# Stick-breaking attention on one core: the diagonal mask moved from a matmul into the scan, and eight small products moved from VectorE to ScalarE

## The chip, the cores and the metric

The kernel runs on one core of a Trainium2 chip, in one launch. The metric is the device time in microseconds. Three runs of the kernel before took 1741.11, 1733.97 and 1735.38 us, so the median is 1735.38 us.

The engines are named as the profile names them: PE is TensorE, with PEld for its weight loads; DVE is VectorE; ACT is ScalarE; POOL is GpSimd; SP is SyncE, which issues the DMAs here. `DVEq` or `SPq` is the part of an engine that issues instructions.

## The reference, cut to what matters

One decoder layer over 2048 positions of 1024 features, all in float32. A conditioning vector `c` gives shift, scale and gate; the input is normalised and modulated, projected to 4096 columns, and goes through eight heads of stick-breaking attention and four heads of differential attention. Each head's output is gated, everything is joined, projected back and added to `x`.

```python
mod = c @ w_ada + b_ada                       # 3 x 1024: shift, scale, gate
h = rmsnorm(x, norm_g) * (1 + scale) + shift

# stick-breaking head, query t, key s:
z = (q @ k.T) / 8
mask = s < t                                  # strictly causal
log_1m = where(mask, log_sigmoid(-z), 0)
rem = reverse_cumsum(log_1m) - log_1m         # sum over s < j < t
a = where(mask, exp(log_sigmoid(z) + rem), 0)
out = a @ v
```

So the weight of key `s` is sigmoid(z) at `s` times the product of sigmoid(-z) over all keys strictly between `s` and `t`. Keys at `t` and behind it have weight zero.

## The kernel before, in words

**Precision.** Each matmul operand is split into a rounded part (`hH`, `wh`, `aH`: fp32r) and the rest (`hL`, `wl`, `aL`), and each product is three matmuls (`mm3`, L381 to L383). Scores are built from stored high and low parts of q and k in two matmuls (L547).

**Start.** The 1024 features are taken in eight blocks `k` of 128. For each block DVE forms 128 values of scale and 128 of shift as dot products of rows of `w_ada` with `c` (`ada_block`, L179, two instructions of 512 columns for each 128 values). Then `gmul[k] = (1 + scale) * norm_g` (L1015) is made on DVE. PE transposes the normalised `x` (L304), ACT multiplies by `gmul` and adds the shift (L310), ACT rounds that to `hH` (L311), POOL (for `k` from 1 to 6) or DVE (0 and 7) takes the rest `hL` (L312), and PE adds block `k` into four projection tiles `ps_p` and `ps_k` (12 matmuls of 512 columns).

**Stick-breaking heads.** The sequence is done in two halves of 1024 queries. For each head, a block `i` of 128 queries is a row of work over `L = (i + 1) * 128` keys, taken in segments of up to 512 keys from the last to the first (`front`, L653 on). The last segment, called `top` in the code, holds the diagonal block as its last 128 columns. A segment is: the scores into a PSUM tile `ps_z`; a sigmoid of them by ACT into `s` (L680); a sigmoid of their negative by ACT in place (L681); on DVE a scan from right to left that multiplies up the second sigmoid into `u` (L684), begun at one in the top segment and at the next segment's left end in the others; and on POOL `s[j] *= u[j + 1]` (L688). For the diagonal, a third matmul (L550, `identr` times `maskr`) adds -1e30 to the scores of keys at or behind the query: there the first sigmoid is zero and the second is one. `maskr` is built once on POOL in `more_constants`. With eight heads and 16 blocks there are 128 such rows, 320 segments and 128 mask matmuls. For two rows together `s` is then transposed by PE (L583), split, and multiplied with `v` (L665, L666).

**Order.** A planner weaves the attention steps with the steps of the projections (lists `A` and `P`, costs beside each step), and a scheduler then sets the order on each engine. The `big` pool has six buffers of 2048 columns for `u` and `s` (and, in the differential heads, `e0` and `e1`). `dist` is a table in SBUF, with zero or negative distances and -1e30, that the differential heads add; the scan names it as its second input and passes it by.

Of the kernel before, what the change touches and what calls it, by code (L numbers as in the profile page):

```python
# [8 lines left out]
F32R = mybir.dt.float32r  # L9
I32 = mybir.dt.int32  # L10
AF = mybir.ActivationFunctionType
ALU = mybir.AluOpType
# [4 lines left out]
T = 2048  # L17
# [7 lines left out]
OUT_SCALE = 0.8  # L25
KAPPA_CAP = 2.0 ** 100
NBIG = 6
MASKED = -1e30
NSTG = 8
WINDOW = 17.0  # L30
QK_DELAY = 3
# [15 lines left out]
def build(ctx: ExitStack, tc, xT, xN, cT, cK, normg, w_adaT, b_ada, w_in, qg, kg, lam4, subg, w_out,  # L47
          identd, distd, outT):
    nc = tc.nc
# [12 lines left out]
    def ctile(shape, name, dt=F32):  # L62
        return cpool.tile(shape, dt, name=name, tag=name)
# [16 lines left out]
    identr = ctile([128, 128], "ident", F32R)  # L80
# [9 lines left out]
    ngt = ctile([128, KT], "ngt")  # L90
# [1 line left out]
    qgt = ctile([128, 1], "qgt")  # L92
    kgt = ctile([128, 1], "kgt")
    sgt = ctile([128, 1], "sgt")
    dist = ctile([128, T], "dist")
    maskr = ctile([128, 128], "maskr", F32R)
    qgain = ctile([128, NDF], "qgain")
    subg8 = ctile([128, 1], "subg8")
    ldot = ctile([128, 2], "ldot")
# [3 lines left out]
    def more_constants():  # L103
        nc.sync.dma_start(qgt, qg)
        nc.sync.dma_start(kgt, kg)
        nc.sync.dma_start(sgt, subg)
        tmp0 = ppool.tile([128, 512], F32, name="tmp0", tag="stg", bufs=NSTG)
        lamt = tmp0[:, 0:256].rearrange("p (f d) -> p f d", d=64)
        nc.sync.dma_start(lamt, lam4.unsqueeze(0).broadcast_to([128, 4, 64]))
        for h in range(NDF):  # L110
            nc.gpsimd.tensor_scalar(out=qgain[:, h:h + 1], in0=qgt, scalar1=0.125 / SLOPES[h],
                                    scalar2=None, op0=ALU.mult)
        nc.gpsimd.tensor_scalar(out=subg8, in0=sgt, scalar1=OUT_SCALE, scalar2=None, op0=ALU.mult)
        lprod = tmp0[:, 256:384].rearrange("p (f d) -> p f d", d=64)
        nc.vector.tensor_tensor(out=lprod, in0=lamt[:, 0::2, :], in1=lamt[:, 1::2, :], op=ALU.mult)
        nc.vector.reduce_sum(out=ldot, in_=lprod, axis=AX.X)
        nc.scalar.activation(lexp, ldot, AF.Exp)
        nc.vector.tensor_tensor(out=neglam, in0=lexp[:, 1:2], in1=lexp[:, 0:1], op=ALU.subtract)
        nc.vector.tensor_scalar(out=neglam, in0=neglam, scalar1=-LAM_INIT, scalar2=None, op0=ALU.add)
        mk = tmp0[:, 384:512]  # L120
        nc.gpsimd.memset(mk, 0.0)
        nc.gpsimd.affine_select(out=mk, in_=mk, pattern=[[-1, 128]], compare_op=ALU.is_gt,
                                fill=MASKED, base=0, channel_multiplier=1)
        nc.gpsimd.tensor_copy(maskr, mk)


    def dtile(shape, name):
# [29 lines left out]
    def after(ins, f):  # L157
        with tc.issue_after(ins.ins):
            return f()
# [8 lines left out]
    mod = ctile([128, 24], "mod")  # L168
# [5 lines left out]
    def ada_block(third, j, wt, cb):  # L174
        m = third * 8 + j
        part = col.tile([128, 1], F32, name="part", tag="adas", bufs=1)
        for i, (ini, acc) in enumerate(((badat[:, m:m + 1], part), (part, mod[:, m:m + 1]))):
            ws = wt[:, i * 512:i * 512 + 512]
            nc.vector.tensor_tensor_reduce(out=ws, in0=ws, in1=cb[i], scale=1.0, scalar=ini,  # L179
                                           op0=ALU.mult, op1=ALU.add, accum_out=acc)  # L180
# [34 lines left out]
    gmul = ctile([128, KT], "gmul")  # L215
# [86 lines left out]
    def turn(ps, xn, k):  # L302
        for t in range(4):
            nc.tensor.transpose(ps[:, t * 128:(t + 1) * 128],  # L304
                                xn[k // 4][t][:, (k % 4) * 128:(k % 4) * 128 + 128], ident)
# [169 lines left out]
    last_pe = [None]  # L475
# [64 lines left out]
                              src[u % 2, :, :, qs:qs + 256].rearrange("l p t -> p l t"))  # L540
        return qt

    def scores(q, kch, i, k0, w, diag=None):
        ps = zps.tile([128, 512], F32, name="ps_z", tag="z")
        tl = slice((i % 2) * 128, (i % 2) * 128 + 128)
        for pt in range(2):
            last_pe[0] = nc.tensor.matmul(ps[:, :w], lhsT=q[:, pt, tl], rhs=kch[k0 // 512][:, :w],  # L547
                                          start=pt == 0, stop=pt == 1 and diag is None)
        if diag is not None:
            last_pe[0] = nc.tensor.matmul(ps[:, diag:diag + 128], lhsT=identr, rhs=maskr, start=False,  # L550
                                          stop=True)
        return ps

    def segs(n, ext):
        return [(o, min(512, n - o), min(512, n - o)) for o in range(0, n, 512)]
# [91 lines left out]
    class SBHead(Head):  # L647
# [20 lines left out]
        def front(self, i, A):  # L668
            steps = []
            tiles = {}  # L670

            def step(c0, w, we, first):
                self.open()
                q = self.get_q(i // 2)
                if first:
                    tiles["u"], tiles["s"] = self.row("u", i), self.row("s", i)
                u, s = tiles["u"], tiles["s"]
                dg = i * 128 - c0
                ps = scores(q, self.kch, i, c0, we, dg if 0 <= dg < w else None)
                nc.scalar.activation(s[:, c0:c0 + w], ps[:, :w], AF.Sigmoid, scale=0.125)  # L680
                nc.scalar.activation(ps[:, :w], ps[:, :w], AF.Sigmoid, scale=-0.125)  # L681
                top = c0 + w == L
                ur = ps[:, :w][:, ::-1]
                nc.vector.tensor_tensor_scan(out=u[:, c0:c0 + w][:, ::-1], data0=ur, data1=dist[:, :w],  # L684
                                             initial=1.0 if top else u[:, c0 + w:c0 + w + 1],
                                             op0=ALU.mult, op1=ALU.bypass)
                m = w - 1 if top else w
                nc.gpsimd.tensor_tensor(out=s[:, c0:c0 + m], in0=s[:, c0:c0 + m],  # L688
                                        in1=u[:, c0 + 1:c0 + m + 1], op=ALU.mult)

            L = (i + 1) * 128
            ext = (i // 2 + 1) * 256
            for si, (c0, w, we) in enumerate(reversed(segs(L, ext))):
                steps.append((2 * w / 960, lambda c0=c0, w=w, we=we, f=si == 0: step(c0, w, we, f)))

            def mid():
                A[0] = tiles["s"]
            return steps, (0.2, mid)
# [313 lines left out]
    turn(xps[0], xn0, 0)  # L1012
    for k in range(KT):
        after(rs0, lambda: ada_block(1, k, wa[(1, k)], cb))
        nc.vector.scalar_tensor_tensor(out=gmul[:, k:k + 1], in0=mod[:, 8 + k:9 + k], scalar=1.0,  # L1015
                                       in1=ngt[:, k:k + 1], op0=ALU.add, op1=ALU.mult)
        after(rs0, lambda: ada_block(0, k, wa[(0, k)], cb))
        make_h(k, 0, xps[k % 2], *hs[0], k in POOL_H)
        if k + 1 < KT:
            turn(xps[(k + 1) % 2], xn0, k + 1)  # L1020
        for w, pst in ((w_q, pq), (w_k, pk)):
            for s in range(2):
                wh, wl = w[k]
                ws = slice(s * 128, s * 128 + 128)
                mm3(pst[s], wh[:, ws], wl[:, ws], hs[0][0][(k, 0)], hs[0][1][(k, 0)], k == 0,
                    k == KT - 1)
# [220 lines left out]
def _layout(inputs):  # L1247
    import numpy as np
    a = {k: np.asarray(v) for k, v in inputs.items()}
    p = np.arange(128)  # L1250
    j = np.arange(T)
    rel = (j[None, :] - 1920 - p[:, None]).astype(np.float32)
    return {
        "xT": np.ascontiguousarray(a["x"][0].T),
        "xN": np.ascontiguousarray(a["x"][0]),
        "cT": np.ascontiguousarray(a["c"][0]),
        "cK": np.ascontiguousarray(a["c"][0].reshape(KT, 128).T),
        "normg": np.ascontiguousarray(a["norm_g"][0].reshape(KT, 128).T),
        "w_adaT": np.ascontiguousarray(a["w_ada"][0].T),
        "b_ada": np.ascontiguousarray(a["b_ada"][0].reshape(24, 128).T),  # L1260
        "w_in": np.ascontiguousarray(a["w_in"][0]),
        "qg": np.ascontiguousarray(np.tile(a["q_norm_g"][0], 2).reshape(128, 1)),
        "kg": np.ascontiguousarray(np.tile(a["k_norm_g"][0], 2).reshape(128, 1)),
        "lam4": np.ascontiguousarray(np.stack([a["lambda_q1"][0], a["lambda_k1"][0],
                                               a["lambda_q2"][0], a["lambda_k2"][0]])),
        "subg": np.ascontiguousarray(a["subln_g"][0].reshape(128, 1)),
        "w_out": np.ascontiguousarray(a["w_out"][0]),
        "ident": np.eye(128, dtype=np.float32),
        "dist": np.where(rel <= 0, rel, np.float32(-1e30)).astype(np.float32),
    }  # L1270


# [18 lines left out]
```

## Time and profile before

| what | before |
|---|---|
| median of 3 runs | 1735.38 us |
| the profiled execution, whole | 1733.63 us |
| its span, first to last instruction | 1731.8 us |
| mean granted TensorE clock | 0.996 |
| PE busy | 1669.4 us, 96% |
| DVE busy | 1236.3 us, 71% |
| ACT busy | 1000.3 us, 58% |
| POOL busy | 836.6 us, 48% |
| DMA | 268.15 MB, mean 155 GB/s |

The span is the time inside which all rows below lie; the profiled execution took 1.8 us more. The profile counts an instruction as busy from its start to the end of its result, and matmuls are pipelined, so the next one starts before the last has ended. What a matmul takes from the engine is therefore read from the distance between starts.

### The profile page before, as it was taken

The page shows a single profiled execution, that of the slowest core. Times are in us where ns is not written, and L with a number is a line of the kernel's source. Part 1 is how long each engine was busy: PE and PEld are TensorE (multiplying, and loading weights), DVE is VectorE, ACT ScalarE, POOL GpSimd, SP SyncE. Part 2 cuts the span into 40 slices and gives each one's busy share as a digit, 9 for nine tenths or more (in the row PEclk, how much of TensorE's full clock was granted, in tenths as well). Part 3 has the DMA queues.
Part 4 walks back from the last instruction along what each step waited for, and adds up shares of the span by engine and source line. Part 5 has one row for each costly group of instructions (what it writes and reads, how often), then busy time and mean ns, then how long its engine had stood idle before and what let it go on. Part 6 is the DMA issues. An engine that isn't in the chain of part 4 may idle for free.

```text
span 1731.8 us, 31619 instructions
## 1 busy us (share of the span) xinstructions
PE 1669.4 (96%) x10816; PEld 1494.2 (86%) x10816; DVE 1236.3 (71%) x2556; ACT 1000.3 (58%) x2027; POOL 836.6 (48%) x1266
## 2 busy tenths in 40 slices
PE   7899899999999999999999999999999999999999
PEld 6688688899999889878898889899998978888887
DVE  6626455766566887767787887788788889888741
ACT  4625555456555454766776777687665645554521
POOL 3325455457545644655565465576332353223553
PEclk9999999999999999999999999999999999999999
DMA  9585767534654975434432332234433566443264
GB/s 348 167 236 162 199 201 240 184 108 117 200 169 142 286 211 163 149 107 117 128 116 89 102 98 86 80 104 126 132 99 108 164 208 200 128 134 129 88 220 149
DMA packets 212690, 268.15 MB, mean 155 GB/s; under 512 B 21424, under 2 KB 136368, under 8 KB 212400
## 3 DMA queue, kind: packets, MB, share of 16 engines
q1 hardware_dynamic: 212528, 266.12, 50.5%
q8 instruction: 86, 1.41, 0.3%
q14 instruction: 76, 0.62, 0.1%
HBM read 186.34 MB, written 79.69 MB: 154 GB/s over the span
## 4 chain that ended last, share of the span: by engine, by line
PE 64%; DVE 8%; DMA 4%; issue 4%; POOL 3%; ACT 3%; SPq 1%; DVEq 0%; ACTq 0%; POOLq 0%
PE ps_z L547 10%; PE ps_t L583 8%; PE ps_n L381 5%; PE ps_n L383 5%; PE ps_n L382 5%; PE ps_p L381 4%; PE ps_p L383 4%; PE ps_p L382 4%; PE av L666 3%; PE av L665 3%; PE ps_o L381 3%; PE ps_o L382 3%; PE ps_o L383 3%; DMA xt<-in_xT 2%; DVE u L684 1%
## 5 line engine op out<-in xcount | busy, mean ns | idle before, releaser
L688 POOL TENSOR_TENSOR s<-s,u 128x512 f32<-128x512 f32 (+4 forms) x320 | 306.2, 959 | 274.1 <-DVE u L684 238.5
L547 PE MATMUL ps_z<-kc,qc 128*128 128x512 f32 (+3 forms) x1280 | 358.8, 374 | 10.5 <-DVE u L684 7.9
L589 ACT CAST aH<-ps_t 128x512 fp32r<-128x512 f32 (+1 forms) x432 | 240.7, 567 | 168.7 <-PE ps_t L583 165.1
L590 DVE TENSOR_TENSOR aL<-ps_t,aH 128x512 fp32r<-128x512 f32 (+1 forms) x432 | 276.7, 650 | 79.7 <-ACT aH L589 78.3
L369 POOL TENSOR_TENSOR wl<-raw,wh 128x512 fp32r<-128x512 f32 x168 | 224.5, 1344 | 128.1 <-ACT wh L365 118.3
L381 PE MATMUL ps_n<-wh,hH 128*128 128x256 f32 x960 | 275.2, 287 | 2.5 <-DVE sl L392 2.2
L383 PE MATMUL ps_n<-wh,hL 128*128 128x256 f32 x960 | 271.6, 283 | 0.0
L382 PE MATMUL ps_n<-wl,hH 128*128 128x256 f32 x960 | 271.2, 283 | 0.4 <-POOL wl L369 0.4
L684 DVE TENSOR_TENSOR_SCAN u<-ps_z,u,dist 128x512 f32<-128x512 f32 x192 | 245.7, 1280 | 32.2 <-ACT ps_z L681 26.5
L780 ACT ACTIVATE e<-e,nm 128x1024 f32<-128x1024 f32 (+4 forms) x192 | 172.1, 898 | 125.3 <-DVE nm L778 121.0
L547 PEld LDWEIGHTS ps_z<-kc,qc 128*128 128x128 f32 x1280 | 210.8, 190 | 37.4 <-DVE u L684 13.4
L766 DVE CUSTOM_DVE_ANT_0 e<-ps_z,dist 128x512 f32<-128x512 f32 (+3 forms) x320 | 186.6, 604 | 50.8 <-PE ps_z L547 44.0
L680 ACT ACTIVATE s<-ps_z 128x512 f32<-128x512 f32 (+3 forms) x320 | 172.9, 540 | 77.4 <-PE ps_z L547 39.2
L381 PE MATMUL ps_p<-hH,wh 128*128 128x512 f32 x480 | 192.2, 406 | 6.1 <-ACT hH L311 6.1
L382 PE MATMUL ps_p<-hL,wh 128*128 128x512 f32 x480 | 190.5, 397 | 0.8 <-POOL hL L312 0.6
L383 PE MATMUL ps_p<-hH,wl 128*128 128x512 f32 x480 | 189.3, 394 | 0.0
L381 PEld LDWEIGHTS ps_n<-wh,hH 128*128 128x128 f32 x960 | 182.6, 191 | 7.0 <-DVE sl L392 2.5
L382 PEld LDWEIGHTS ps_n<-wl,hH 128*128 128x128 f32 x960 | 182.7, 191 | 3.7 <-POOL wl L369 0.6
L383 PEld LDWEIGHTS ps_n<-wh,hL 128*128 128x128 f32 x960 | 182.8, 191 | 1.8
L681 ACT ACTIVATE ps_z<-ps_z 128x512 f32<-128x512 f32 (+3 forms) x320 | 173.5, 542 | 0.0
L583 PE MATMUL ps_t<-ident,s 128*128 128x128 f32 x1088 | 168.6, 275 | 4.6 <-DVE aL L590 4.3
L665 PE MATMUL av<-aH,vc 128*128 128x256 f32 x576 | 160.7, 290 | 7.9 <-ACT aH L589 6.7
(190 smaller groups left out, 3456.0 us busy)
## 6 DMA issues: line engine op xcount, KB each, us to landing
qc<-qst SPq DMA_DIRECT2D x256, 128.0 KB, 3.1
raw<-in_w_in SPq DMA_DIRECT2D x120, 256.0 KB, 3.2
kc<-kst SPq DMA_DIRECT2D x96, 256.0 KB, 3.5
vc<-vst SPq DMA_DIRECT2D x48, 256.0 KB, 3.0
vc<-vdt SPq DMA_DIRECT2D x48, 256.0 KB, 3.6
raw<-in_w_out SPq DMA_DIRECT2D x48, 256.0 KB, 3.4
wada<-in_w_adaT SPq DMA_DIRECT2D x16, 512.0 KB, 8.3
qst<-sh SPq DMA_DIRECT2D x64, 128.0 KB, 2.5
```

Of the source, the lines that this page charges most:

```text
L369: (eng or nc.gpsimd).tensor_tensor(out=wl, in0=raw, in1=wh.bitcast(F32), op=ALU.subtract)
L381: nc.tensor.matmul(ps, lhsT=aH, rhs=bH, start=first, stop=False)
L382: nc.tensor.matmul(ps, lhsT=aH, rhs=bL, start=False, stop=False)
L383: nc.tensor.matmul(ps, lhsT=aL, rhs=bH, start=False, stop=last)
L547: last_pe[0] = nc.tensor.matmul(ps[:, :w], lhsT=q[:, pt, tl], rhs=kch[k0 // 512][:, :w], start=pt == 0, stop=pt == 1 and diag is None)
L583: nc.tensor.transpose(tp[:, pos * 256 + t * 128:pos * 256 + t * 128 + 128], A[t][0][:, sb * 128:sb * 128 + 128], ident)
L589: nc.scalar.copy(aH[:, f0:], tp[:, f0:])
L590: nc.vector.tensor_tensor(out=aL[:, f0:], in0=tp[:, f0:], in1=aH[:, f0:].bitcast(F32), op=ALU.subtract)
L665: nc.tensor.matmul(o, lhsT=v, rhs=aH, start=st, stop=False)
L684: nc.vector.tensor_tensor_scan(out=u[:, c0:c0 + w][:, ::-1], data0=ur, data1=dist[:, :w], initial=1.0 if top else u[:, c0 + w:c0 + w + 1], ...
L688: nc.gpsimd.tensor_tensor(out=s[:, c0:c0 + m], in0=s[:, c0:c0 + m], in1=u[:, c0 + 1:c0 + m + 1], op=ALU.mult)
L766: nc.vector.tensor_tensor_reduce(out=e[m][:, c0 + o:c0 + o + w], in0=ps[:, :w], in1=dist[:, d0:d0 + w], scale=1.0, scalar=-3e38, op0=ALU.a ...
```

## The change

The mask matmul, its constant and the three POOL instructions that build it go. The scan of a top segment gets a second operation: after the multiplication it takes the maximum with an input, and it begins at zero instead of one. That input is read backwards from `dist`, which is 128 columns longer; those columns are an identity matrix. From the right, the product stays zero until the diagonal, where the maximum with the identity's one makes it one, and from there it is the product as before. The other columns of `dist` that are read are zero or negative and change nothing. So `u` is zero behind the diagonal, and `s * u` is zero there whatever `s` is. The very last column of a row has no `u` to its right: ACT now leaves it out (511 columns of 512, and so on), and POOL writes a zero there (a memset of 128 x 1, one for each of the 128 rows). Apart from that, the eight `gmul` products are made by ACT (identity of scale times `ngt` plus `ngt`) instead of by DVE.

```diff
-    dist = ctile([128, T], "dist")
-    maskr = ctile([128, 128], "maskr", F32R)
+    dist = ctile([128, T + 128], "dist")
...
-        mk = tmp0[:, 384:512]
-        nc.gpsimd.memset(mk, 0.0)
-        nc.gpsimd.affine_select(out=mk, in_=mk, pattern=[[-1, 128]], compare_op=ALU.is_gt,
-                                fill=MASKED, base=0, channel_multiplier=1)
-        nc.gpsimd.tensor_copy(maskr, mk)
...
-    def scores(q, kch, i, k0, w, diag=None):
+    def scores(q, kch, i, k0, w):
...
-                                          start=pt == 0, stop=pt == 1 and diag is None)
-        if diag is not None:
-            last_pe[0] = nc.tensor.matmul(ps[:, diag:diag + 128], lhsT=identr, rhs=maskr, start=False,
-                                          stop=True)
+                                          start=pt == 0, stop=pt == 1)
...
-                dg = i * 128 - c0
-                ps = scores(q, self.kch, i, c0, we, dg if 0 <= dg < w else None)
-                nc.scalar.activation(s[:, c0:c0 + w], ps[:, :w], AF.Sigmoid, scale=0.125)
+                ps = scores(q, self.kch, i, c0, we)
+                top = c0 + w == L
+                m = w - 1 if top else w
+                nc.scalar.activation(s[:, c0:c0 + m], ps[:, :m], AF.Sigmoid, scale=0.125)
+                if top:
+                    nc.gpsimd.memset(s[:, L - 1:L], 0.0)
...
-                nc.vector.tensor_tensor_scan(out=u[:, c0:c0 + w][:, ::-1], data0=ur, data1=dist[:, :w],
-                                             initial=1.0 if top else u[:, c0 + w:c0 + w + 1],
-                                             op0=ALU.mult, op1=ALU.bypass)
+                nc.vector.tensor_tensor_scan(out=u[:, c0:c0 + w][:, ::-1], data0=ur,
+                                             data1=dist[:, T + 128 - w:T + 128][:, ::-1] if top else dist[:, :w],
+                                             initial=0.0 if top else u[:, c0 + w:c0 + w + 1],
+                                             op0=ALU.mult, op1=ALU.max if top else ALU.bypass)
...
-        nc.vector.scalar_tensor_tensor(out=gmul[:, k:k + 1], in0=mod[:, 8 + k:9 + k], scalar=1.0,
-                                       in1=ngt[:, k:k + 1], op0=ALU.add, op1=ALU.mult)
+        nc.scalar.activation(gmul[:, k:k + 1], mod[:, 8 + k:9 + k], AF.Identity,
+                             scale=ngt[:, k:k + 1], bias=ngt[:, k:k + 1])
...
-        "dist": np.where(rel <= 0, rel, np.float32(-1e30)).astype(np.float32),
+        "dist": np.concatenate([np.where(rel <= 0, rel, np.float32(-1e30)),
+                                j[None, :128] == p[:, None]], axis=1).astype(np.float32),
```

The scheduler sets the order anew. Three places show what stands where. The first is DVE at the start, where block `k` = 3 of the modulation is formed (`ISA` with `mod` as its result ends 128 values; `wada` is a tile of `w_ada` rows, `ps_cb` holds `c`). Before:

```order
L179 ISA wada_255,part_463<-wada_255,ps_cb_213,badat_109 128x512
L179 ISA part_463 128x1
L179 ISA wada_255,mod_195<-wada_255,ps_cb_214,part_463 128x512
L179 ISA mod_195 128x1
L1015 SCALAR_TENSOR_TENSOR gmul_196<-mod_195,ngt_111 128x1
L179 ISA wada_255,part_467<-wada_255,ps_cb_213,badat_109 128x512
L179 ISA part_467 128x1
L179 ISA wada_255,mod_195<-wada_255,ps_cb_214,part_467 128x512
```

DVE at the same place in the changed kernel:

```order
L174 ISA wada_254,part_462<-wada_254,ps_cb_212,badat_109 128x512
L174 ISA part_462 128x1
L174 ISA wada_254,mod_194<-wada_254,ps_cb_213,part_462 128x512
L174 ISA mod_194 128x1
L174 ISA wada_254,part_466<-wada_254,ps_cb_212,badat_109 128x512
L174 ISA part_466 128x1
L174 ISA wada_254,mod_194<-wada_254,ps_cb_213,part_466 128x512
```

The product `gmul` no longer stands between the values of scale and those of shift; on ACT it now stands ahead of L310 of the same block, eight times.

The second is PE where the first three rows of the first head are scored, between matmuls of a projection. Before:

```order
L382 MATMUL ps_p<-hL_0_558,wh 128x512
L547 MATMUL ps_z<-kc,qc 128x128 x2
L550 MATMUL ps_z<-maskr,ident 128x128
L547 MATMUL ps_z<-kc,qc 128x256 x2
L550 MATMUL ps_z<-maskr,ident 128x128
L547 MATMUL ps_z<-kc,qc 128x384 x2
L550 MATMUL ps_z<-maskr,ident 128x128
L383 MATMUL ps_p<-hH_0_557,wl 128x512
```

PE at the same place in the changed kernel:

```order
L377 MATMUL ps_p<-hL_0_557,wh 128x512
L542 MATMUL ps_z<-kc,qc 128x128 x2
L542 MATMUL ps_z<-kc,qc 128x256 x2
L542 MATMUL ps_z<-kc,qc 128x384 x2
L378 MATMUL ps_p<-hH_0_556,wl 128x512
```

Only the mask matmuls have gone there; elsewhere in the stick-breaking stretches steps have traded places with their neighbours, and the differential heads and the end of the program stand as before.

The third is POOL in the second half, where row `s_11956` (before) or `s_11950` (changed kernel) ends a head and `s_12071` or `s_12065` begins the next one. Before:

```order
L688 TENSOR_TENSOR s_11874<-s_11874,u_11873 128x383
L688 TENSOR_TENSOR s_11874<-s_11874,u_11873 128x512 x2
L688 TENSOR_TENSOR s_11956<-s_11956,u_11955 128x511
L688 TENSOR_TENSOR s_11956<-s_11956,u_11955 128x512 x2
L714 TENSOR_TENSOR ot_12017<-ot_12017,gt_12015 64x512
L688 TENSOR_TENSOR s_12071<-s_12071,u_12070 128x127
```

POOL at the same place in the changed kernel:

```order
L683 TENSOR_TENSOR s_11868<-s_11868,u_11867 128x383
L683 TENSOR_TENSOR s_11868<-s_11868,u_11867 128x512 x2
L675 MEMSET s_11950 128x1
L675 MEMSET s_12065 128x1
L683 TENSOR_TENSOR s_11950<-s_11950,u_11949 128x511
L683 TENSOR_TENSOR s_11950<-s_11950,u_11949 128x512 x2
L709 TENSOR_TENSOR ot_12011<-ot_12011,gt_12009 64x512
L683 TENSOR_TENSOR s_12065<-s_12065,u_12064 128x127
```

The memset of the next row stands ahead of the products of the row before it, and it waits for PE to have transposed what its buffer held last.

## Rows read from the trace of the kernel before

**Rows 1.** The page: engine, busy us (share of the span), instructions.

```profile
PE 1669.4 (96%) x10816; PEld 1494.2 (86%) x10816; DVE 1236.3 (71%) x2556; ACT 1000.3 (58%) x2027; POOL 836.6 (48%) x1266
```

**Rows 2.** Two stick-breaking stretches: length, busy us per engine, clock, DMA share, GB/s.

```profile
200.00:420.00 220.00, 208.64 (x1372) 187.83 (x1370) 134.80 (x210) 121.26 (x257) 119.29 (x151) 1.00 0.57 170
860.00:1060.00 200.00, 198.56 (x1292) 177.83 (x1290) 157.38 (x191) 145.30 (x294) 111.02 (x107) 1.00 0.33 102
```

**Rows 3.** Who PE waited for: us in total, times, longest us.

```profile
PE ps_z L547 <- DVE u L684: 7.9, 15, 0.8
PE ps_t L583 <- DVE aL L590: 6.7, 10, 2.4
PE av L665 <- ACT aH L589: 6.7, 6, 1.4
```

**Rows 4.** The mask matmul by form: count, busy us, mean ns, idle us before.

```profile
L550 PE MATMUL ps_z<-maskr,ident 128*128 128x128 f32 x128 | 30.4, 237 | 0.0
```

**Rows 5.** PE's timeline around a mask matmul: start us, us, instruction.

```profile
118.53 0.22 PE L550 MATMUL ps_z<-maskr,ident 128*128 128x128 f32 x1
118.59 0.45 PE L383 MATMUL ps_p<-hH,wl 128*128 128x512 f32 x1
118.88 0.39 PE L381 MATMUL ps_p<-hH,wh 128*128 128x512 f32 x1
119.10 0.40 PE L382 MATMUL ps_p<-hL,wh 128*128 128x512 f32 x1
```

**Rows 6.** PE's timeline behind scores without a mask matmul.

```profile
901.10 0.63 PE L547 MATMUL ps_z<-kc,qc 128*128 128x512 f32 x2
901.57 0.28 PE L382 MATMUL ps_n<-wl,hH 128*128 128x256 f32 x1
901.69 0.27 PE L383 MATMUL ps_n<-wh,hL 128*128 128x256 f32 x1
```

**Rows 7.** The product gmul: its durations (min/median/max ns), and DVE and POOL once.

```profile
L1015 DVE SCALAR_TENSOR_TENSOR gmul<-mod,ngt x8: 159/1286/1292, 17.0 to 47.3; 128x1 f32<-128x1 f32 x8
25.50 1.29 DVE L1015 SCALAR_TENSOR_TENSOR gmul<-mod,ngt 128x1 f32<-128x1 f32 x1
25.48 1.29 POOL L312 TENSOR_TENSOR hL<-xh,hH 128x512 fp32r<-128x512 f32 x1 [5.88 <-ACT hH L311]
```

**Rows 8.** PE's timeline at the start: transposes, first matmuls of blocks 2 and 7.

```profile
29.18 0.66 PE L304 MATMUL ps_x<-ident,xn 128*128 128x128 f32 x4
...
29.83 0.73 PE L381 MATMUL ps_p<-hH,wh 128*128 128x512 f32 x2
...
51.99 0.73 PE L381 MATMUL ps_p<-hH,wh 128*128 128x512 f32 x2 [1.23 <-ACT hH L311]
```

**Rows 9.** The tile wada up to 60 us: its issues on SP, and issue to landing.

```profile
L172 SPq DMA_DIRECT2D wada<-in_w_adaT x16: 328/340/668, 6.6 to 29.0; - x16
...
DMA to landing us min/median/max: 4.8/8.3/9.5
```

**Rows 10.** DVE by form: a top scan, and a plain subtraction of the same shape.

```profile
L590 DVE TENSOR_TENSOR aL<-ps_t,aH 128x512 fp32r<-128x512 f32 x336 | 225.4, 680 | 65.7 <-ACT aH L589 64.8
...
L684 DVE TENSOR_TENSOR_SCAN u<-ps_z,dist 128x512 f32<-128x512 f32 x32 | 38.9, 1215 | 8.8 <-ACT ps_z L681 6.3 <-PE ps_t L583 2.4
```

**Rows 11.** A small memset on POOL, and a small activation on ACT.

```profile
L1278 POOL MEMSET const-float32-0.0<- 128x1 f32 x1 | 0.1, 98 | 0.2 <-issue 0.2
L117 ACT ACTIVATE lexp<-ldot 128x2 f32<-128x2 f32 x1 | 0.2, 203 | 2.8 <-DVE ldot L116 2.8
```

**Rows 12.** What POOL waited for most: us in total, times, longest us.

```profile
POOL s L688 <- DVE u L684: 238.5, 196, 8.1
```

**Rows 13.** Timelines of PE and POOL where a buffer comes free.

```profile
910.88 0.60 PE L583 MATMUL ps_t<-ident,s 128*128 128x128 f32 x4
...
912.25 0.63 POOL L688 TENSOR_TENSOR s<-s,u 128x255 f32<-128x255 f32 x1 [3.22 <-DVE u L684]
```

**Rows 14.** ACT's timeline: an activation that waits for a DMA.

```profile
104.20 0.63 ACT L220 ACTIVATE xacc<-xt 128x512 f32<-128x512 f32 x1 [5.81 <-DMA xt<-in_xT]
```

More of the change, by code (lines that the diff above doesn't have):

```diff
@@ L27 @@
 NBIG = 6
-MASKED = -1e30
 NSTG = 8
@@ L677, in step @@
                 u, s = tiles["u"], tiles["s"]
-                dg = i * 128 - c0
-                ps = scores(q, self.kch, i, c0, we, dg if 0 <= dg < w else None)
-                nc.scalar.activation(s[:, c0:c0 + w], ps[:, :w], AF.Sigmoid, scale=0.125)
+                ps = scores(q, self.kch, i, c0, we)
[4 more added lines that the diff above has]
+                    nc.gpsimd.memset(s[:, L - 1:L], 0.0)
                 nc.scalar.activation(ps[:, :w], ps[:, :w], AF.Sigmoid, scale=-0.125)
-                top = c0 + w == L
                 ur = ps[:, :w][:, ::-1]
-                nc.vector.tensor_tensor_scan(out=u[:, c0:c0 + w][:, ::-1], data0=ur, data1=dist[:, :w],
-                                             initial=1.0 if top else u[:, c0 + w:c0 + w + 1],
-                                             op0=ALU.mult, op1=ALU.bypass)
-                m = w - 1 if top else w
+                nc.vector.tensor_tensor_scan(out=u[:, c0:c0 + w][:, ::-1], data0=ur,
+                                             data1=dist[:, T + 128 - w:T + 128][:, ::-1] if top else dist[:, :w],
+                                             initial=0.0 if top else u[:, c0 + w:c0 + w + 1],
+                                             op0=ALU.mult, op1=ALU.max if top else ALU.bypass)
                 nc.gpsimd.tensor_tensor(out=s[:, c0:c0 + m], in0=s[:, c0:c0 + m],
```

## The prediction

> **What bounds the kernel now.** Read the page's busy line first: PE is busy 96% of the span, DVE 71%, ACT 58%, POOL 48% [rows 1]. A busy share can hide stalls, since a matmul counts as busy until its result is out. So look next at the table by stretch: in a stretch of stick-breaking rows of the first half PE is busy 208.64 of 220 us, in one of the second half 198.56 of 200, DVE 134.80 and 157.38 [rows 2]. Last, who PE waited for: the three largest are 7.9, 6.7 and 6.7 us in the whole run, 31 waits together [rows 3]. PE is the bound, from the first scores to the end, and what leaves its queue shortens the run unless a wait stands right behind it. The other place is the start, up to about 55 us, where PE waits for each block of the modulated input.
>
> **The mask matmuls on PE.** There are 128, with a mean duration of 237 ns [rows 4], but the duration is not the price. The timeline shows one start at 118.53, the next matmul at 118.59 and the one behind that at 118.88 [rows 5]. So the mask matmul holds the queue 0.06 us, and the 512-column matmul behind it needs 0.29 us until the next start where the following one of the same shape needs 0.22 (118.88 to 119.10): another 0.07. Behind plain scores nothing is stretched: at 901.57 a 256-column matmul gives way after 0.12 us [rows 6], about half of what 512 columns take. [...] That is 0.13 us, with rounding at four ends; I take 0.12, so 128 x 0.12 = 15.4 us. What PE saves just ahead of a wait, the wait eats: with 31 waits I take off 31 x 0.12 = 3.7. That leaves 11.7 us. Bounds: 15.4 where no wait eats any, and 128 x 0.06 = 7.7 less a quarter for waits, 5.8, where the stretch stays and goes to the matmul before.
>
> [...]
>
> **The product gmul at the start.** It works on one column, but its median is 1286 ns against a least of 159 [rows 7]. The reason stands beside it: at 25.50 it begins while POOL runs `hL` from 25.48 for 1.29 us, and it ends with it. While it stands there, the shift of the same block, next on DVE, is late; ACT's L310 waits for that shift, and PE for ACT. PE's first matmul of block 2 starts at 29.83 and that of block 7 at 51.99, so one block takes 22.16 / 5 = 4.43 us; at block 7 PE had waited 1.23 us [rows 8]. PE's own work for a block is four transposes, 0.66 us [rows 8], and 12 matmuls at 0.22 us [rows 5], 3.3 us. DVE without the product needs about 4.43 - 1.29 = 3.1 us a block. So PE becomes the pace, with 4.43 - 3.3 = 1.13 us gained on each of five blocks: 5.6 us. The loads allow it: the last `wada` issue is at 29.0, and with a landing after at most 9.5 us all are there at 38.5 [rows 9], where the new pace wants the last block at about 45. On ACT the product costs about 0.2 us by a small activation [rows 11]; ACT waits for DVE there anyway. I take 5.0 of the 5.6, since behind the blocks come loads that no engine paces: at 104.20 ACT has waited 5.81 us for a DMA of `xt`, with other work queued behind it [rows 14]. Bounds: 5.6, and 0 where those loads take back all of it.
>
> [...]
>
> **The scan with a maximum.** No row shows a scan whose second operation does anything. A top scan of 512 takes 1215 ns, a subtraction of the same shape 680 [rows 10], so the scan already pays nearly two steps for each element, as a loop through two operations would, although the second is passed by. I take the price of the maximum as zero. Bounds: below nothing there is no reason; above, a third step, (1215 / 2) = 0.6 us per 512 columns. The 32 top segments of each width hold 32 x (128 + 256 + 384 + 512) = 40,960 columns, 80 times 512, so 48 us on DVE.
>
> **POOL's memsets.** 128 at about 0.1 us [rows 11] are 12.5 us on POOL, which waited 238.5 us for scans in these rows [rows 12]; they fit there. Where that cover is gone they cost at most the 12.5. They also add a wait: in the second half the memset of the next row stands ahead of the products of the row before and waits for PE to have transposed its buffer's last content. Behind it stand those products, and PE's next transposes wait for these. The trace shows when that buffer comes free: four transposes start at 910.88 and end at 911.48, and the product behind them starts at 912.25, since its scan needs the same buffers [rows 13]. So the memset has 0.8 us before the product is due. I take nothing; up to 0.1 us a row, 64 rows, 6 us above, and nothing below. The mask's three POOL instructions (once) and one column less for ACT are nothing either way: both engines wait there.
>
> **The sum.** 11.7 + 5.0 = 16.7 us off the profiled execution, 1733.63, is 1716.9. It stands 1.75 us below the median of the runs, so the forecast for a median is 1718.6. The 1.8 us around the span stay.
>
> **The rivals.** First, the start's gain is given back, so that only PE's 11.7 stays: 1735.38 - 11.7 = 1723.7. For it: the first scores come at 118, behind stores, reloads and the DMA waits of rows 14. Against it: most of those loads are issued when PE or DVE is done with something, and would shift along.
>
> Second, the rows of attention don't run at PE's pace but at that of the chain from ACT's sigmoids over the scan to POOL's product; PE would only wait more, and the start's 5.0 is all: 1730.4. For it: POOL's 238.5 us of waiting for scans, and 11 us of PE idle in 220 in the first half [rows 2]. Against it: PE's named waits are only 21 us in all, and the chain gets shorter by 0.06 us a row too, since ACT's sigmoid waited for the mask.
>
> Third, on the other side: the maximum makes top scans slower by a third step, 48 us on DVE in the stretches where it is busy 61% to 79%. If all of it ends up in PE's waits, the time is 1735.38 - 16.7 + 48 = 1766.7; it decides (slower by over 0.5%) once PE waits for more than 25 of the 48. Against it: the scan's rate already is that of two operations.
>
> [...]
>
> Fourth, the change doesn't do what it says because the new order, made for the changed set of instructions, loses elsewhere what it gains: I put 10 us on that, 1728.6. For it: steps have traded places in the stick-breaking stretches. Against it: most move by one or two matmuls.
>
> **How the numbers follow.** Forecast 0.62, 1711 to 1726 by the bounds (15.4 + 5.6 = 21.0 with 3 us for waits that vanish below; 5.8 + 3.0 above). First rival 0.12, second 0.12, third 0.06, fourth 0.08. For 8 in 10 the range reaches from 1710 to 1731, over the first, second and most of the fourth. Half a per cent, 8.7 us, is what a measurement of this kernel can tell from none; the border is 1726.7. Faster by more: the forecast, most of the first rival, a little of the fourth: 0.74. Within: the second, most of the fourth, part of the third: 0.19. Slower: most of the third and bad orders: 0.07.
>
> **What would show it.** The PE work without L550 has the same spacing, and matmuls behind scores no longer show 0.29 us. At the start, blocks follow each other on PE every 3.3 us, DVE's dot products have no gap of 1.2 us, and the first scores start before 114 us instead of about 118. A top scan of 512 still takes about 1.2 us. POOL's memsets take 0.1 us, and POOL's products start no later behind their scans. I am wrong if PE's waits for DVE or ACT grow by more than the 3.7 us taken off, if the first scores still start near 118, or if the top scans take 1.8 us.

## The result, and the profile after

The changed kernel took 1727.47 us in the median of six runs (1724.80 to 1730.57), the kernel before 1736.70 us in six runs beside them. The ratio is 0.9945, with an interval from 0.9927 to 0.9963: 9.2 us faster. Six more runs of the changed kernel (e9) gave 0.9952 (0.9933 to 0.9971) beside runs of the kernel before. The forecast was 1718.6 us, so a little over half of the forecast gain arrived. The profiled execution took 1727.51 us, with a span of 1725.7 us.

The first fence is the page of the changed kernel, the line that answers to [rows 1].

```profile
PE 1659.9 (96%) x10688; PEld 1482.5 (86%) x10688; DVE 1231.1 (71%) x2548; ACT 1005.4 (58%) x2035; POOL 847.2 (49%) x1391
```

The 128 mask matmuls are gone from PE, ACT has eight instructions more and DVE eight less, POOL has 125 more. Next, two stretches of the changed kernel, moved by about 10 us against [rows 2]: length, busy us of PE, PEld, DVE, ACT and POOL, granted clock, DMA share, GB/s.

```profile
190.00:410.00 220.00, 210.64 (x1338) 187.96 (x1338) 138.41 (x211) 124.72 (x261) 121.26 (x192) 0.98 0.59 173
850.00:1050.00 200.00, 195.52 (x1240) 171.77 (x1239) 155.69 (x190) 142.36 (x290) 112.68 (x130) 1.00 0.32 100
```

In the first stretch PE is as busy as before. In the second it isn't: it is idle 200 - 195.52 = 4.5 us, where the kernel before was idle 1.4 us [rows 2]. The clock column matters too: 0.98 in the first stretch, where the kernel before showed 1.00. Now the start, on PE of the changed kernel: first matmuls of blocks 2 and 7 (start us, us, instruction), and the eight `gmul` products, now on ACT (duration ns min/median/max, first and last start).

```profile
29.45 0.71 PE L376 MATMUL ps_p<-hH,wh 128*128 128x512 f32 x2
...
45.53 0.61 PE L376 MATMUL ps_p<-hH,wh 128*128 128x512 f32 x2
```

```profile
L1010 ACT ACTIVATE gmul<-mod,ngt x8: 382/387/389, 17.9 to 41.6; 128x1 f32<-128x1 f32 x8
```

Five blocks take 45.53 - 29.45 = 16.1 us, 3.2 us each, where they took 4.43 [rows 8]. The product takes 0.39 us on ACT, and nobody waits for it there. Then DVE's top scan and POOL's memsets of the changed kernel, by form (count, busy us, mean ns, idle us before and what ended it), and POOL's wait at the memsets.

```profile
L679 DVE TENSOR_TENSOR_SCAN u<-ps_z,dist 128x512 f32<-128x512 f32 x32 | 38.9, 1217 | 12.5 <-ACT ps_z L676 12.3
```

```profile
L675 POOL MEMSET s<- 128x1 f32 x128 | 10.4, 100 | 35.4 <-PE ps_t L575 34.2
```

```profile
POOL s L675 <- PE ps_t L575: 34.2, 12, 7.0
```

The scan with the maximum takes 1217 ns, without it 1215 [rows 10]. The memsets take 0.1 us each, and twelve of them wait, up to 7.0 us. Whether that wait costs anything the page can't say; run e11 below does. Last, PE at the place of [rows 5], in the changed kernel:

```profile
110.93 0.97 PE L542 MATMUL ps_z<-kc,qc 128*128 128x128 f32 x6
111.74 0.39 PE L378 MATMUL ps_p<-hH,wl 128*128 128x512 f32 x1
111.97 0.39 PE L376 MATMUL ps_p<-hH,wh 128*128 128x512 f32 x1
112.20 0.40 PE L377 MATMUL ps_p<-hL,wh 128*128 128x512 f32 x1
```

The matmul behind the scores needs 0.23 us until the next start, as the one behind it does (111.97 to 112.20); the 0.29 us are gone. The first scores start at 110.93 instead of 117.50. PE's named waits for DVE and ACT come to 51.0 us in the whole run, where they were 50.4, so the prediction's sign of being wrong (more than 3.7 us more) doesn't show in them.

### The profile page after: what moved, and what is told of

Same layout as the page of the kernel before. It is cut to its first block, busy times and chain, and to the rows that moved or that the text cites. A ratio compares the mean times of both kernels' runs of the same rounds, so it can differ in the third digit from the quotient of the medians.

```text
span 1725.7 us, 31468 instructions
## 1 busy us (share of the span) xinstructions
PE 1659.9 (96%) x10688; PEld 1482.5 (86%) x10688; DVE 1231.1 (71%) x2548; ACT 1005.4 (58%) x2035; POOL 847.2 (49%) x1391
## 4 chain that ended last, share of the span: by engine, by line
PE 68%; DVE 11%; DMA 7%; issue 5%; ACT 4%; POOL 4%; SPq 1%; DVEq 0%; ACTq 0%; POOLq 0%
PE ps_z L542 11%; PE ps_t L575 7%; PE ps_n L376 6%; PE ps_n L378 6%; PE ps_n L377 6%; PE ps_p L376 4%; PE ps_p L377 4%; PE ps_p L378 4%; DVE u L679 3%; PE ps_o L377 3%; PE ps_o L376 3%; PE ps_o L378 3%; PE av L658 3%; PE av L657 3%; DMA xt<-in_xT 3%
## 5 line engine op out<-in xcount | busy, mean ns | idle before, releaser
L673 ACT ACTIVATE s<-ps_z 128x512 f32<-128x512 f32 (+4 forms) x320 | 169.2, 543 | 67.2 <-PE ps_z L542 48.9
L676 ACT ACTIVATE ps_z<-ps_z 128x512 f32<-128x512 f32 (+3 forms) x320 | 168.2, 538 | 1.8
```

## The experiments

**How the runs are compared.** Each run lists its mean granted clock. Over the 173 runs of all kernels in these experiments, a run whose mean clock is 0.001 lower is 1.03 us longer (a fit with one level for each kernel; 0.88 to 1.19). The kernels differ by a few us and the runs of one kernel by ten, so the table gives each kernel's time at a clock of 0.994 from this fit, with its 95% interval, beside the plain median. "Old" is the order of instructions that the kernel before has, "new" that of the changed kernel.

| kernel | order | runs | median us | mean clock | at 0.994, us |
|---|---|---|---|---|---|
| before (e1 and beside all others) | old | 85 | 1737.8 | 0.9936 | 1737.2 ± 0.5 |
| e2, gmul on ACT alone | old | 9 | 1728.4 | 0.9942 | 1729.8 ± 1.4 |
| e5, masks gone alone | old | 5 | 1730.1 | 0.9928 | 1728.9 ± 1.9 |
| e8, e10, the whole change | old | 12 | 1723.5 | 0.9939 | 1723.1 ± 1.2 |
| changed kernel, with e9 | new | 12 | 1728.6 | 0.9910 | 1726.1 ± 1.3 |
| e3, without gmul on ACT | new | 12 | 1735.9 | 0.9927 | 1732.8 ± 1.2 |
| e11, memsets moved | new | 8 | 1729.6 | 0.9910 | 1726.6 ± 1.6 |
| e6, masks put back | new | 12 | 1739.1 | 0.9916 | 1735.1 ± 1.3 |
| e7, the same work | a third | 12 | 1734.2 | 0.9904 | 1730.9 ± 1.3 |
| e4, without memsets | a fourth | 6 | 1727.7 | 0.9938 | 1727.7 ± 1.7 |

**The kernel before again.** My theory after this profile was that the gain at the start had arrived, that the mask matmuls gave little, and that a denser PE had lost some 5 us to a lower clock. No edit.

> The kernel before, unchanged, run again: its own granted clock is wanted. In the profiled runs the clock was 0.996 before and 0.993 after; the six runs of after lay between 0.990 and 0.993. Theory A (the lower clock belongs to the change, a denser PE): all runs of the kernel before show 0.995 or more, and the time stays at 1736.7 us within 0.2%. Rival B (how often the clock falls is chance in either kernel): the runs of the kernel before spread over 0.990 to 0.996 like those of after, and the slower of them are those with the lower clock.

Median 1736.56 us of 12 runs, clock from 0.989 to 0.998. The kernel before falls to low clocks too, and its runs with a low clock are the long ones: the five at 0.993 or less took 1738.98 to 1742.89 us, the seven at 0.995 or more 1731.37 to 1736.98. So the time of a single profiled run may not be read for a few us: that of the kernel before, at 0.996, was a lucky one. Theory A is out as it stands: low clocks aren't the change's alone. Whether they are more frequent in the changed kernel is taken up at the end.

**The parts alone.** e2 is the kernel before with the `gmul` products on ACT:

```diff
-        nc.vector.scalar_tensor_tensor(out=gmul[:, k:k + 1], in0=mod[:, 8 + k:9 + k], scalar=1.0,
-                                       in1=ngt[:, k:k + 1], op0=ALU.add, op1=ALU.mult)
+        nc.scalar.activation(gmul[:, k:k + 1], mod[:, 8 + k:9 + k], AF.Identity,
+                             scale=ngt[:, k:k + 1], bias=ngt[:, k:k + 1])
```

> The kernel before with the eight gmul products on ACT, mask matmul and scan as they were; PE, POOL and SP run in the same order as before. Theory A (the start gave what it was forecast, and it lasts to the end): 4.9 us less, about 1731.8 us, first scores at about 111 us. Rival 1 of the prediction (the start's gain is given back to loads behind it): first scores near 111, but the offset to the kernel before is gone by 300 us, time within 1 us of 1736.7. If a kernel with less waiting at the start pays in granted clock, the clock falls to about 0.993 here too.

Ratio 0.9956 (0.9938 to 0.9974): 8.8 us by medians, 7.4 at equal clock, more than the 4.9 expected. These rows are the scores in the kernel before and then in e2, first at their beginning and then at their end (duration ns, first and last start us, forms):

```profile
L547 PE MATMUL ps_z<-kc,qc x11: 220/335/499, 117.5 to 124.8; 128*128 128x128 f32 x4, 128*128 128x512 f32 x3, 128*128 128x256 f32 x2, 128*128 128x384 f32 x2
L547 PE MATMUL ps_z<-kc,qc x28: 333/396/496, 1602.9 to 1623.5; 128*128 128x512 f32 x24, 128*128 128x384 f32 x4
```

```profile
L547 PE MATMUL ps_z<-kc,qc x14: 220/320/477, 111.6 to 124.1; 128*128 128x128 f32 x4, 128*128 128x256 f32 x4, 128*128 128x512 f32 x4, 128*128 128x384 f32 x2
L547 PE MATMUL ps_z<-kc,qc x22: 333/396/500, 1601.4 to 1618.1; 128*128 128x512 f32 x20, 128*128 128x384 f32 x2
```

The first scores come 5.9 us earlier, the last 5.4 us. The start's gain lasts, and the first rival is out. For e3 the same edit is undone in the changed kernel:

> The changed kernel with the gmul products back on DVE: mask by the scan alone; PE and POOL run in the order of the changed kernel. Theory A (start 4.9, the mask matmuls net 4.3 of the 11.7 forecast): about 1732.4 us, clock between 0.990 and 0.993, first scores near 117.5. Rival (the mask matmuls gave their 11.7 and the start gave nothing in the end): about 1727 here, as in the changed kernel with both. Rival 4 (the new order costs): can't be told apart here, the order stays.

1735.87 us, ratio 0.9983 (0.9968 to 0.9999): 1.4 us by medians, 4.4 at equal clock. The theory's number was 1732.4, the rival's 1727; neither is met by the median, and at equal clock (1732.8) it is the theory's. Set beside the changed kernel instead, e3 prices `gmul` a second time, in the new order: 6.7 ± 1.8 us. The expected clock, 0.990 to 0.993, came (0.9927). So 128 matmuls less had brought little. Either they are worth little, or something in the new order takes it back.

**The memsets left out.** In e4 POOL's memset line is deleted and ACT writes the whole top segment, so the last column of each row is left unmasked.

> The changed kernel without POOL's 128 memsets and without their waits for PE's transposes; ACT writes the full width of a top segment, so the last column of each row is left unmasked. Theory A (the memsets cost nothing, as the products behind them never started later than their scans let them): 1727.5 us as the changed kernel, within 2 us. [...] The order on the engines is set anew here, so a change of 2 us either way would only measure that.

1727.74 us, as the changed kernel. But the scheduler made a fourth order of it, so it tells little; at equal clock it is 1.6 us above the changed kernel, with less to do, though within the intervals.

**The price of a mask matmul, with the order held.** The next pair changes the instructions after the scheduler is done, so that nothing else moves. In e5 the mask matmuls leave the kernel before (their semaphore update goes to the matmul ahead of them), and the diagonal is left unmasked. In e6 matmuls of the same shape are put into the changed kernel behind the top segments' scores.

```diff
     with tile.TileContext(nc, schedule_with_timeline_sim=True) as tc:
         build(tc, *args)
+    drop_masks(nc)            # e5: instructions named in MASKS leave PE's list
+    add_masks(nc, WARMS[0])   # e6: identr x identr, 128 columns, behind the top segments' scores
```

> The kernel before with its 128 mask matmuls taken out after the scheduler has set the order: every engine runs the order of the kernel before, the scan, the memsets and the gmul products are as before; the diagonal is left unmasked. It gives the price of the mask matmuls alone. So far the part with the scan alone took 64 rows of the first half from 340 to 328 us at full clock (0.18 us for each matmul), those of the second half from 531 to 531 (0.01 each), and the stages behind gave back 3. Theory C (that is the matmul's price where it stands: much in the first half, nothing in the second): first half -10 to -12, second half 0 to -2, about 1727 us at the clock of 0.994, and as much as 1732 if the clock falls to 0.991. Theory D (the price is 0.12 as forecast in both halves, and the new order loses the rest): -8 in each half, nothing given back, about 1721.

> The changed kernel with 128 matmuls of the mask's shape put in behind the top segments' scores after the scheduler has set the order (identity times identity, which only touches masked scores); all else in the order of the changed kernel. Theory C: 8 to 10 us slower than the changed kernel, 1736 to 1737, almost all of it in the first half. Theory D: 15 us slower, 1742, half in each half. If the clock falls because the mask matmuls are gone, it rises to 0.994 here, against 0.992 without them.

Without the masks, old order: 1730.09 us, ratio 0.9953 (0.9938 to 0.9967), 8.0 us by medians, 8.3 ± 2.0 at equal clock. With them, new order: 1739.10 us, 9.0 ± 1.8 more than the changed kernel at equal clock. Both are near the 8 to 10 that theory C gives for e6, and far from D's 15 and 16: 0.065 to 0.07 us for each matmul, not 0.12. But theory C also said that the order didn't matter, and there it is wrong: the new order with masks and `gmul` on ACT takes 1735.1, the old one with the same matmuls (e2) 1729.8. The clock did not rise with the masks back (0.9916). At the place of [rows 5] the timeline of e5 shows this:

```profile
118.33 0.97 PE L548 MATMUL ps_z<-kc,qc 128*128 128x128 f32 x6
119.14 0.39 PE L384 MATMUL ps_p<-hH,wl 128*128 128x512 f32 x1
119.37 0.39 PE L382 MATMUL ps_p<-hH,wh 128*128 128x512 f32 x1
```

Three scores and the matmul behind them take 119.37 - 118.33 = 1.04 us; with three masks they took from 117.50, the start of the first scores, to 118.88, 1.38 us. That is 0.11 us a mask here, near the forecast 0.12. It is so nearly everywhere: PE's instructions in the kernel before and in e5 are the same, in the same order, but for the masks, so the two profiles can be set beside each other matmul by matmul. At 117 of the 127 masks that both profiles show at full clock no wait stands beside the mask, and there e5 saves 0.11 us in the median. All 127 places together give 11.6 us, and 8.3 ± 2.0 are left in the end. So the local price is right, and about four tenths of it is taken back, partly on the spot and partly further behind.

**Another order of the same work.** In e7 the changed kernel's order is set with mask matmuls in it (identity times identity), which are taken out afterwards.

> The changed kernel, but its order set as if the mask matmuls still stood there; they are taken out afterwards. Same work as the changed kernel, another order. Theory C (the order matters little): 1727.5 within 2 us. Theory D (the order of the changed kernel loses up to 10 us): another order can differ by 5 us or more, in the stick-breaking rows of the second half; without the 128 memsets an order that was set anew took 538 us at full clock there, where the changed kernel takes 529.

1734.15 us; at equal clock 4.8 ± 1.8 us slower than the changed kernel, with the same instructions. The order is worth as much as half of all mask matmuls.

**The whole change in the old order.** So e8 takes the kernel before, with `gmul` on ACT and the maximum in the scan, lets the scheduler set the order with the masks in it, takes them out, and puts each memset behind the product of its top segment. PE then runs the order of the kernel before. Some memsets of the first half lie on a column of another row in e8, so its result is not the kernel's; e10 has each on its own row.

```diff
+    drop_masks(nc)
+    add_memsets(nc, MEMSET[0])   # POOL: a memset right behind each top segment's product, with no wait
```

> The whole change, but in the order of the kernel before: the order is set with mask matmuls in it, which are then taken out, and each memset is put on POOL right behind the product of its top segment, where it waits for nothing. PE runs the order of the kernel before without L550. Theory D (the mask matmuls are worth about 8 us as measured with the order kept, the start 7, and the new order of the changed kernel costs about 4): 1736.8 - 7 - 8 = 1722 us, 3 to 5 us below the changed kernel. Rival (scan and memsets, not the order, cost the 4): 1726, as the changed kernel. Theory E (the order sets how often the clock falls): mean clock 0.9935, as the kernels in the old order have, not 0.992.

> The changed kernel, unchanged, beside the run above on the same chip: 1727.5 us within 2, mean clock 0.992. Theory E: the clock stays below 0.993 in the mean. Rival: it spreads around 0.9935 like the kernel before, and the six runs so far were chance.

> As the run e8 (the whole change in the order of the kernel before, each memset right behind the product of its top segment), with the memset now at the last column of its own row: in e8 the memsets of the first half's rows that are the second of their buffer lay on a column of the other row. Time as e8: 1723.5 us within 2, clock 0.9935 or more, 3 to 7 us below the changed kernel.

e8 took 1723.48 us, ratio 0.9907 (0.9889 to 0.9926); e10 1723.47, ratio 0.9918 (0.9898 to 0.9938); the changed kernel beside e8 1730.56. So e10 computes what the changed kernel computes and is 4 to 7 us faster, by the median of all twelve runs 5.1. At equal clock 3.0 ± 1.8 of that stay; the rest is clock, 0.9939 against 0.9910.

**The memsets moved, new order held.** e11 is the changed kernel with each memset moved behind its product, after the scheduler.

> The changed kernel with its order kept on every engine, but each memset moved on POOL to right behind the product of its top segment, where it waits for nothing. Theory D (the order of PE, not the memsets' waits, costs the 4 to 7 us between the changed kernel and e8): as the changed kernel, 1727 to 1731 us, clock 0.992 or less. Rival (the memsets that wait for PE's transposes hold POOL's products up): 4 us less or more, 1723 to 1725.

1729.64 us, clock 0.9910. Its memsets have no wait any more:

```profile
L677 POOL MEMSET s<- 128x1 f32 x128 | 12.7, 99 | 0.0
```

The 34.2 us that POOL waited at them are gone, and the time stays: 1726.6 ± 1.6 us at equal clock, against 1726.1 ± 1.3. Neither the memsets nor their waits cost anything; what is left between the changed kernel and e10 is the order. (ACT's sigmoid of a top segment is one column wider in e10; if that costs anything, it costs e10.)

**Where the order loses.** PE's waits for a free `ps_z`, first in the changed kernel, then in e10 (us in total, times, longest us):

```profile
PE ps_z L542 <- DVE u L679: 10.2, 18, 2.6
PE ps_z L542 <- DVE mx L761: 4.0, 4, 2.1
```

```profile
PE ps_z L543 <- DVE u L681: 7.6, 14, 0.8
PE ps_z L543 <- DVE mx L766: 2.3, 4, 0.9
```

In all its waits together PE doesn't lose more in the new order: 61.3 us in the changed kernel, 63.1 in e10. But the longest ones for `ps_z` differ, and they are at two places. PE in the changed kernel, then in e10 (in brackets the wait):

```profile
134.42 0.73 PE L542 MATMUL ps_z<-kc,qc 128*128 128x512 f32 x2 [2.58 <-DVE u L679]
...
1281.60 1.11 PE L542 MATMUL ps_z<-kc,qc 128*128 128x512 f32 x4 [2.12 <-DVE mx L761]
```

```profile
133.97 0.73 PE L543 MATMUL ps_z<-kc,qc 128*128 128x512 f32 x2 [0.43 <-DVE u L681]
...
1279.17 1.81 PE L543 MATMUL ps_z<-kc,qc 128*128 128x512 f32 x6 [0.42 <-DVE mx L766]
```

These are 2.58 + 2.12 - 0.43 - 0.42 = 3.9 us more. Waits of 2.4 to 2.6 us for `u` and of 2.1 us for `mx` stand in all five profiles of the new order, e6 with its mask matmuls among them. In the six of the old order the longest are 0.8 to 1.4 us for `u` (once, in e2, 2.0) and 0.9 for `mx`. The first can be followed on ACT; the changed kernel, then the kernel before:

```profile
129.71 0.63 ACT L673 ACTIVATE s<-ps_z 128x512 f32<-128x512 f32 x1
131.93 0.63 ACT L218 ACTIVATE xsq<-xt 128x512 f32<-128x512 f32 x1 [1.59 <-DMA xt<-in_xT]
132.47 0.58 ACT L676 ACTIVATE ps_z<-ps_z 128x512 f32<-128x512 f32 x1
```

```profile
135.56 0.64 ACT L680 ACTIVATE s<-ps_z 128x512 f32<-128x512 f32 x1
136.05 0.63 ACT L681 ACTIVATE ps_z<-ps_z 128x512 f32<-128x512 f32 x1
137.96 0.63 ACT L223 ACTIVATE xsq<-xt 128x512 f32<-128x512 f32 x1 [1.28 <-DMA xt<-in_xT]
```

In the old order both sigmoids of the segment run, and then ACT waits for a load. In the new one the instruction that waits for the load stands between the two sigmoids, so the second is 2.76 us behind the first instead of 0.49, the scan behind it is late, and PE waits for the scan. At the second place DVE, in the changed kernel, runs two products of the differential heads and a reduction ahead of the maximum (`mx`) that frees `ps_z`; in e10 its products stand elsewhere.

```profile
1277.40 3.21 DVE L804 SCALAR_TENSOR_TENSOR e<-e,kp,e 128x1024 f32<-128x1024 f32 x2
```

That these two waits are what the order costs is not shown: no run takes them out, and around the first nothing is lost in sum. From the 1st to the 201st transpose of `s` on PE the changed kernel takes 253.86 us at a granted clock of 0.98, and e10 253.89 at 0.99. The loss shows most clearly where no such wait stands: from the 401st to the 801st transpose of `s`, in the rows of the second half. All profiles were granted the full clock there, so they can be compared to a few tenths of a microsecond. In order: the kernel before, e10, the changed kernel and e6 (length, busy us of PE, PEld, DVE, ACT and POOL, granted clock, DMA share, GB/s):

```profile
807.73:1066.63 258.90, 256.24 (x1664) 229.02 (x1662) 204.48 (x248) 187.75 (x381) 145.12 (x140) 1.00 0.35 106
801.54:1058.39 256.85, 253.91 (x1631) 225.35 (x1630) 204.17 (x248) 187.74 (x381) 146.55 (x172) 1.00 0.35 107
797.74:1058.48 260.74, 255.37 (x1629) 224.80 (x1628) 204.63 (x249) 186.66 (x381) 148.20 (x173) 1.00 0.35 105
799.36:1062.25 262.89, 258.63 (x1662) 228.75 (x1661) 205.24 (x249) 187.37 (x381) 148.39 (x173) 1.00 0.35 105
```

The stretch has 32 masks (the counts take in matmuls that overlap its ends). With them the old order takes 258.9 to 259.0 us (also in e1 and e2), without them 256.7 to 256.9 (also in e5 and e8). The new order takes 260.7 to 261.1 without masks (also in e3, e9 and e11) and 262.9 with them. So 32 masks cost about 2.1 us here in either order, 0.065 us each as in the whole run, and the new order costs 3.9 us with two matmuls less. PE is idle 5.4 us in place of 2.9, and no wait that the profile names is longer than 1.0 us: the loss is spread over many. Over the rest of the program the new order gains in places and loses in others. This is also why the part with the scan alone seemed to gain nothing in the second half (in the expectation of e5): what the masks give there, the order takes.

## Why the prediction was right in direction and about half right in size

- **The start, 5.0 us: right in mechanism, too small.** Blocks follow each other every 3.2 us as forecast, PE is the pace (busy 15.73 of the 16.08 us of five blocks), and the loads take nothing back. It gave 5.4 to 5.9 us between the traces of the kernel before and e2 and 7.4 ± 1.5 in the runs, where 5.6 was my upper bound. The five blocks alone give 22.16 - 16.08 = 6.1, since PE needs 3.2 us for one and not 3.3; that lies within the interval of the runs. What I took off for the loads behind should have been nothing.
- **The mask matmuls, 11.7 us: too large.** Held in order they are worth 8.3 ± 2.0 and 9.0 ± 1.8 us. The 0.12 us for one is nearly right (0.11 at most places in e5). What stretched the matmul behind a mask no run shows; with the mask gone its 0.29 us are 0.23 (the changed kernel and e5). The step that failed is the term for what is taken back, 31 x 0.12 = 3.7. It counted the waits that the profile names, at one mask each, and should have been about 7 of the 15.4. My lower bound, 5.8, held.
- **The scan at nothing: right,** 1217 against 1215 ns; the third rival is dead. **The memsets at nothing: right,** by e11, although they wait 34.2 us in all.
- **The new order at nothing: wrong, and the largest miss.** It has no term in the sum; the fourth rival had the mechanism at 10 us and 0.08. It costs 3.0 ± 1.8 us at equal clock, 3.9 in one stretch of 260 us alone, and the runs in the new order have a lower clock: over all kernels 0.9916 (44 runs) against 0.9936 (111 runs) in the old one. For the changed kernel alone, 0.9910, it is 0.0026, or 2.7 us by the fit. It isn't the chip: the kernel before, run beside them, had 0.9932 to 0.9939 on each of the four chips of these experiments, and e3, e6, e9 and e11 had less than it on theirs.

The account at the fit's numbers: 16.7 forecast, 2.4 more at the start, 3.4 less from the masks, 1.6 lost where both parts are together in the old order (7.4 + 8.3 is 15.7, measured 14.1, within the intervals), 3.0 for the order at equal clock, 2.7 for its clock. That leaves 8.4 us; the medians of all runs say 9.2. The start's 2.4 us stood against the other misses; that part of the nearness is luck.

The mistake in reasoning was to take "most steps move by one or two matmuls" as evidence that the order costs nothing. A stretch in which it loses 3.9 us eats more than a quarter of the 14.1 us that the change gains in the old order, and no single step in it stands out.

## What to carry to other kernels

Where a scheduler sets the order anew, a change of a few tenths of a per cent is read together with a draw of the order: here the same work took from 1723.1 to 1730.9 us at equal clock in three orders. Measure the edit with the order held (let the scheduler see the old instruction, and take it out afterwards), and then compare the two orders stretch by stretch, between the same instructions and where both were granted the same clock. A wait that is longer than any was before is a place to look at, such as an instruction that waits for a load in the middle of a chain; but it counts only if its stretch is longer too. And compare kernels only with the clock of each run beside its time.

## What the runs showed of the hardware that I had not expected

The mean granted clock of one and the same kernel, before, ranged from 0.989 to 0.998, and with it the time from 1731.37 to 1742.89 us in the runs of e1. Orders of the same work differ in it: 0.9939 in e8 and e10, 0.9910 in the changed kernel, 0.9904 in e7. It isn't the missing mask matmuls: with them put back (e6) the clock is 0.9916, and without them in the old order 0.9939. What it is in an order that lets the clock fall more often, the runs don't show in general. One place can be named: in all five profiles of the new order the clock falls to half at 1283 to 1291 us (in the changed kernel 0.50 from 1283.5 to 1286.0), within 2.1 us of the end of PE's 2.1 us wait for `mx`, so that the granted clock from 1282 to 1295 us is 0.87. In the six of the old order it is 1.00 from 1120 to 1320. The wait alone isn't shown to be the reason: in e7 it stands too, at 1295, and the clock stays at 1.00 behind it.

A two-input product on one column that took 1286 ns on DVE beside POOL takes 387 ns as an activation with scale and bias read from SBUF, more than the 203 ns of the small activation that I had gone by [rows 11].
